# Layer 1's heads: the second map's scores half a step behind the first map's, with the first turns and the values between them

## The chip, the cores and the metric

The kernel runs on one core of one Trainium2 chip. A core has a matrix engine (PE, with its weight loads shown apart as PEld), a vector engine (DVE), a scalar engine (ACT), GpSimd (POOL) and SyncE (SP), which here only issues DMAs. Each engine works off its own list of instructions in order, and the engines wait for each other through semaphores. PE writes its results to eight banks of PSUM, from which DVE and ACT read. The metric is the device time of one execution in microseconds; lower is better.

## The reference

A backbone of two layers over 1024 latent tokens and 256 context tokens of width 1024. Layer 0 is a latent attention and isn't touched here. Layer 1 is a differential attention with 8 heads: each head has two attention maps over the 1280 keys, and one value of width 128.

```
def diff_mixer(h, h_c, rows, need_ctx, layer_idx, w_in, lam, g_sub):
    ...
    def combine(o1, o2, gate):
        o = o1 - lam_full.astype(o1.dtype) * o2
        o = rms_norm(o, g_sub) * (1.0 - lambda_init)
        return gated(o, gate)
    ...
    o1, o1_c = prefix_attention(q[:, :, :, 0:1], k[:, :, :, 0], v, ...)
    o2, o2_c = prefix_attention(q[:, :, :, 1:2], k[:, :, :, 1], v, ...)
```

Behind it come the output projection, a residual and a layer norm.

## The kernel before

Layer 1 runs head by head, and in a head by tiles of 128 query tokens: 8 steps of `step1` for each of the 8 heads. A step works on three tiles at once:

- **Scores** of the current tile (`scores1`, a generator with three parts). The first part computes the first map's scores and the scores of both maps against the context: on PE a bank for the context (four products 256 wide) and two banks of 512 keys (two products each, L1348 and L1349); on DVE the context's maxima (L1361), two maxima (L1365) and their combination (L1367); on ACT three exponentials (L1371) with their sums. The second part does the two 512-key banks of the second map and its three exponentials. The third part is DVE's alone: the sums (L1374), a reciprocal, a factor (L1376), and the **join** of both maps into one (L1377).
- **Turns** of the tile before (`turn1`, three calls): PE transposes the joined map, 4, 4 and 2 blocks of 128 (L1384), ACT rounds them to `ph` (L182) and DVE keeps the remainder as `pl` (L183).
- **Values** of the tile before that (`values1`): 30 products with `ph`, `pl` and the values on PE (L1392 to L1394), then `o` and its square sum on ACT (L1397, L1398), small work on POOL, and a DMA to `o_d`. Head 7 keeps its result in the chip.

Between these parts, `some(side, cost)` lets a generator with other work go on: for heads 0 to 6 the projections of the next head (k, q, then v, each product 256 or 512 wide, recorded at L186 to L188) with their weights (`wx`, `wy`), their rotation (`rsw`, `kr`, `rr`), rounding (`kH`, `kL`, `vh`, `vl`) and gates (`gg`); for head 7 the output projection of finished tiles. The cost counts streamed columns. `at` holds five costs: `SLOT1` is 2900 five times for heads 0 to 6, `SLOTO` is 0 and then 7000 four times for head 7. Head 7 has no side work in its first two steps.

PE's order is the order in which the code is written (a manual schedule for PE alone); the order on DVE, ACT, POOL and SP and the PSUM bank of each tile are chosen by a scheduler when the program is built. `HP` is 0. There are two buffers each of `ph`, `pl` and of the first map's `p0`, one of the second map's `p1`, four of `sm`.

Of the kernel before, what the change touches and what calls it, by code (L numbers as in the profile page):

```python
# [39 lines left out]
HP = 0  # L40
# [14 lines left out]
def hybrid_kernel(  # L55
# [33 lines left out]
    def bank(tag, dt=F32):  # L89
        return banks["pool"].tile([P, 512], dt, tag=tag, bufs=banks[tag], name=nm("ps_" + tag))  # L90
# [5 lines left out]
    def spool(name, **kw):  # L96
        return tc.tile_pool(name=name, bufs=1, reuse_waits="tile", **kw)
# [5 lines left out]
    def rot(pool_, shape, dt, tag, bufs=1, first=False):  # L103

        if not first and (id(pool_), tag) in pre:
            return pre.pop((id(pool_), tag))
        t = pool_.tile(shape, dt, tag=tag, bufs=bufs, name=nm(tag))
        if first:
            pre[id(pool_), tag] = t
        return t  # L110
# [48 lines left out]
    def rstd_of(dst, src, mul, n):  # L159
        pool.tensor_scalar(dst, src, mul, EPS, op0=ALU.mult, op1=ALU.add)  # L160
        pool.tensor_tensor(dst, dst, neghalf[:, :n], op=ALU.pow)
# [7 lines left out]
    hp = p0.enter_context(spool("p0"))  # L169
# [398 lines left out]
    def chain(*gs):  # L568
        for g in gs:
            yield from g  # L570

    def beside_gates():
        with spool("p0side") as sp_:
            for i, _ in enumerate(up_weights(sp_)):
                if i in (1, 3, 5, 7, 9, 13, 17):
                    yield
        with spool("p0side2") as sp_:
            t_ = lambda tag: sp_.tile([P, D], F32, tag=tag, bufs=3, name=nm(tag))
            yield
            yield  # L580
            yield from ada_dve(t_, ((1, 0), (1, 1), (0, 2)))
# [9 lines left out]
    with spool("p0g") as pg:  # L591
        side = beside_gates()
# [384 lines left out]
    def w1(tag):  # L977
        sh, d, b = TAG1[tag]
        return rot(place[tag], sh, d, tag, b)
# [250 lines left out]
    def weave(main, side, at):  # L1230

        for i, v in enumerate(main):
            if i in at:
                next(side, None)
            yield v
        yield from side
# [37 lines left out]
    def prod_q1(h, b, ps=None):  # L1274
        c0, n = CHUNKS[b]
        if ps is None:
            for ps in proj1(n, c0, slice(0, P)):
                yield 3 * n
        rr = w1("rr")
        c = slice(c0, c0 + n)  # L1280
        rope1(ps, n, cosB[:, c], sinB[:, c], rr)
        if b == 0:
            qt1[h] = [w1(f"Q1{m}") for m in range(2)], [w1(f"QS{m}") for m in range(2)]
        q1, qs = qt1[h]

        def fin():
            H, L = w1("kH")[:, :n], w1("kL")[:, :n]
            if b:
                split16(H, L, rr, es1[h])
            else:  # L1290
                act.activation(H, rr, AF.Copy, scale=es1[h])
                pool.tensor_scalar(rr, rr, es1[h], None, op0=ALU.mult)
                pool.tensor_tensor(L, rr, H, op=ALU.subtract)
            for m in range(2):
                r = slice(m * HD, m * HD + HD)
                dmv(qs[m][:HD, c], H[r, :])
                dmv(qs[m][HD:, c], H[r, :])
                dmv(q1[m][:HD, c], L[r, :])
                dmv(q1[m][HD:, c], L[r, :])

        later.append(fin)
        yield 0
# [85 lines left out]
    def values1(h, t, ph, pl, sm):  # L1388
        vh, vl = vt[h]
        ps = bank("b")[:, :P]  # L1390
        for kc in range(NT):
            pe.matmul(ps, ph[:, kc, :], vh[:, kc, :], start=kc == 0, stop=False)  # L1392
            pe.matmul(ps, ph[:, kc, :], vl[:, kc, :], start=False, stop=False)
            pe.matmul(ps, pl[:, kc, :], vh[:, kc, :], start=False, stop=kc == NT - 1)  # L1394
        o, o2, ss = w1("o1"), w1("o2"), w1("ss")
        pool.tensor_tensor(sm[:, 5:6], sm[:, 2:3], us1[h], op=ALU.mult)  # L1396
        act.activation(o, ps, AF.Copy, scale=sm[:, 5:6])  # L1397
        act.activation(o2, o, AF.Square, accum_out=ss[:, 0:1])  # L1398
        rstd_of(ss[:, 1:2], ss[:, 0:1], 1.0 / P, 1)
        if h == H1 - 1:  # L1400
            oo, g = og[t]
            c = slice(h * P, (h + 1) * P)
            dve.scalar_tensor_tensor(oo[:, c], o, ss[:, 1:2], g[:, c], op0=ALU.mult, op1=ALU.mult)
            return
        pool.tensor_scalar(o, o, ss[:, 1:2], None, op0=ALU.mult)
        sp.dma_start(o_d[1][t * P:(t + 1) * P, h * P:(h + 1) * P], o)
# [148 lines left out]
    def some(gen, cost):  # L1555

        credit[0] += cost
        while credit[0] > 0:
            v = next(gen, None)
            if v is None:  # L1560
                credit[0] = 0
                return
            credit[0] -= v

    with tc.manual_schedule(engines={ENG[c] for c in MAN1}):
        for _ in prod_q1(0, 0, made.pop("q")):
            pass
        later.pop()()
        for _ in chain(prod_k1(0, made), prod_q1(0, 1),
                       weave(prod_v1(0), prod_w(1, 0), WAT[1])):  # L1570
            while later:
                later.pop(0)()
        joined, turned = [], []

        def step1(cur, side, at):

            with tc.high_priority(HP):
                if cur:
                    S = scores1(*cur)
                    next(S)  # L1580
            some(side, at[0])
            with tc.high_priority(HP):
                if cur:
                    next(S)
                if turned:
                    values1(*turned.pop(0))
            some(side, at[1])
            pc = None
            if joined:
                c_, pc, sm = joined.pop(0)  # L1590
                ph, pl = w1("ph"), w1("pl")
                turned.append((*c_, ph, pl, sm))
            for (k0, n), v in zip(((0, 4), (4, 4), (8, 2)), at[2:]):
                if pc is not None:
                    with tc.high_priority(HP):
                        turn1(pc, ph, pl, k0, n)
                some(side, v)
            if cur:
                with tc.high_priority(HP):
                    joined.append((cur, *next(S)))  # L1600
            for _ in range(len(later)):
                later.pop(0)()

        def v_last(h):
            while later:
                later.pop(0)()
            out_early()
            yield from weave(prod_v1(h), chain(*[out_w1(k, lambda: w1("ws")) for k in range(NSP, NOW)],
                                               *[out_pre(k) for k in range(NOW, KT)]), range(1, 36, 2))

        g1 = gate_row1()
        part = lambda h: (v for _, v in zip(range(6 if h else 0), g1))
        early = lambda h: out_w1(h - 3, lambda: w1("ws")) if 3 <= h < 3 + NSP else iter(())
        for h in range(H1):
            last = h == H1 - 1
            if not last:
                G = chain(weave(weave(chain(prod_k1(h + 1), prod_q1(h + 1, 0), prod_q1(h + 1, 1)), part(h), (1, 6, 11, 16, 21, 26)),
                                prod_w(h + 1, 1), WAT[0]),
                          weave(weave(prod_v1(h + 1), early(h), (5, 15)), prod_w(h + 2, 0), WAT[1]) if h + 2 < H1 else v_last(h + 1))
            else:  # L1620
                while later:
                    later.pop(0)()
                out_open()
            for t in range(SEQ // P):
                if last:
                    if t >= 2:
                        out_load(t)
                    G = weave(out_tile1(t - 2), out_turns(t - 1), (9, 12)) if t >= 2 else iter(())
                    if t == 2:
                        G = chain(out_turns(0), G)  # L1630
                    credit[0] = 0
                step1((h, t), G, SLOT1 if not last else SLOTO)
                if last:
                    for _ in G:
                        pass
            for _ in G:
                pass
        for t in range(SEQ // P - 2, SEQ // P):
            G = weave(out_tile1(t), out_turns(t + 1), (9, 12))
            credit[0] = 0  # L1640
            step1(None, G, SLOTO)
            for _ in G:
                pass
# [74 lines left out]
```

## Time and profile before

| | us |
|---|---|
| three runs, median | 1769.6 |
| lowest and highest | 1768.27 and 1771.5 |
| the profiled execution's span, from its first to its last instruction | 1767.7 |
| its heads 0 to 6 of layer 1 | some 947 to 1600 |
| its head 7 and the end | some 1600 to 1767.7 |

The profile is of one execution. Its page gives the span and no other time of that execution; the median of the runs stands 1.9 us above the span. A row of a group gives the line, the engine, what is written and read, how many instructions there are, their busy time together, the mean in ns, and the engine's idle time ahead of them with what ended it. A row of a timeline gives the start, the duration, the engine and the line, and in square brackets an idle time ahead of it. Matmuls are pipelined: a 256-wide one is shown with 0.27 us, but the next starts 0.11 us later.

### The profile page before, as it was taken

What the parts mean: (1) busy time and instruction counts of PE and PEld (TensorE: products, weight loads), DVE (VectorE), ACT (ScalarE), POOL (GpSimd) and SP (SyncE); (2) the same over time, 40 slices, a digit from 0 to 9 for tenths busy, and PEclk for the clock granted to TensorE, in tenths of its full rate; (3) what the DMA queues carried; (4) which work ended last, traced back from release to release, by engine and by line L of the source; (5) the groups of instructions that cost most, each with busy time, mean ns of one, the idle gap of its engine ahead of it and who ended that gap; (6) DMA issues with size and microseconds to landing.
All of it is one profiled execution on the core that took longest, in us unless ns stands there. A gap on an engine that the chain in (4) does not pass through costs nothing. (4 is left out here: it accounts for less than half of the span.)

```text
span 1767.7 us, 36788 instructions
## 1 busy us (share of the span) xinstructions
PE 1660.4 (94%) x14564; PEld 1231.8 (70%) x14564; DVE 1224.6 (69%) x2037; ACT 1118.5 (63%) x2235; POOL 821.9 (46%) x740
## 2 busy tenths in 40 slices
PE   7999989999999998899999999999999999987998
PEld 6999956556666655577867676767676767666876
DVE  7658666565565666646856778787878787878664
ACT  3551177777777778845635676767676767758542
POOL 1432147667767776845552323241424233354454
PEclk9999999999999999999999999999999999999999
DMA  8258520110111122245522222231212222142331
GB/s 308 81 152 259 166 68 21 43 44 22 42 46 25 39 57 62 65 168 196 167 96 64 80 68 80 67 81 55 60 51 63 60 58 75 32 125 66 112 108 72
DMA packets 111225, 154.84 MB, mean 88 GB/s; under 512 B 13415, under 2 KB 84679, under 8 KB 111054
## 3 DMA queue, kind: packets, MB, share of 16 engines
q1 hardware_dynamic: 102654, 144.90, 27.3%
q10 hardware_dynamic: 8400, 7.61, 1.3%
q8 instruction: 114, 1.87, 0.4%
q14 instruction: 57, 0.47, 0.1%
HBM read 98.65 MB, written 27.07 MB: 71 GB/s over the span
## 5 line engine op out<-in xcount | busy, mean ns | idle before, releaser
L780 POOL TENSOR_TENSOR pl<-p,ph 128x1024 f16<-128x1024 f32 (+1 forms) x176 | 364.3, 2076 | 148.4 <-ACT ph L779 122.6
L1371 ACT ACTIVATE p<-ps_b,mx 128x512 f32<-128x512 f32 (+1 forms) x384 | 230.2, 617 | 58.9 <-DVE mx L1367 57.4
L778 ACT ACTIVATE p<-ps_a,esc 128x1024 f32<-128x1024 f32 (+1 forms) x176 | 189.0, 1074 | 94.8 <-PE ps_a L836 88.8
L760 DVE TENSOR_REDUCE mx<-ps_a 128x1 f32<-128x1024 f32 x128 | 155.3, 1222 | 129.9 <-PE ps_a L758 129.8
L779 ACT CAST ph<-p 128x1024 f16<-128x1024 f32 (+1 forms) x176 | 177.1, 1006 | 5.5
L1365 DVE TENSOR_REDUCE mx<-ps_b 128x1 f32<-128x512 f32 x256 | 164.9, 680 | 0.7 <-PE ps_b L1349 0.7
L849 PE MATMUL ps_d<-Vh,pl 128*128 128x65 f16 x1344 | 146.0, 194 | 4.4 <-POOL pl L780 4.4
L846 PE MATMUL ps_d<-Vh,ph 128*128 128x65 f16 x1344 | 148.2, 195 | 0.0
L848 PE MATMUL ps_d<-Vl,ph 128*128 128x64 f16 x1344 | 147.0, 193 | 0.0
L846 PEld LDWEIGHTS <-ph 128*128 128x128 f16 x1344 | 123.3, 97 | 18.1 <-issue 4.9
L848 PEld LDWEIGHTS <-ph 128*128 128x128 f16 x1344 | 124.0, 98 | 12.2 <-issue 0.3
L1348 PE MATMUL ps_b<-KS,QS 128*128 128x512 f16 (+1 forms) x384 | 126.5, 347 | 5.9 <-DVE pl L183 2.9
L1349 PE MATMUL ps_b<-KS,Q 128*128 128x512 f16 (+1 forms) x384 | 129.7, 347 | 0.0
L834 PE MATMUL ps_a<-qH,KH 100*128 100x512 f16 x320 | 121.9, 381 | 7.8 <-ACT p L778 3.5
L1396 POOL TENSOR_TENSOR sm<-sm,us 128x1 f32<-128x1 f32 x64 | 18.5, 289 | 234.3 <-DVE sm L1375 221.2
L849 PEld LDWEIGHTS <-pl 128*128 128x128 f16 x1344 | 123.2, 97 | 5.8 <-POOL pl L780 5.8
L1384 PE MATMUL ps_b<-idr,p 128*128 128x128 f32 x640 | 103.8, 278 | 24.2 <-ACT p L1371 6.2
L183 DVE SCALAR_TENSOR_TENSOR pl<-ps_b,lcf,ph 128x512 f16<-128x512 f32 (+1 forms) x192 | 116.9, 653 | 11.2 <-ACT ph L182 11.2
L182 ACT ACTIVATE ph<-ps_b,lcf 128x512 f16<-128x512 f32 (+1 forms) x192 | 115.2, 647 | 13.9 <-PE ps_b L1384 13.8
L835 PE MATMUL ps_a<-qH,KL 96*128 96x512 f16 x320 | 121.8, 381 | 0.0
L836 PE MATMUL ps_a<-qL,KH 96*128 96x512 f16 x320 | 121.2, 379 | 0.0
L1384 PEld LDWEIGHTS ps_b<-idr,p 128*128 128x128 f32 x640 | 78.2, 143 | 49.0 <-ACT p L1371 11.6
(438 smaller groups left out, 5290.7 us busy)
## 6 DMA issues: line engine op xcount, KB each, us to landing
ws<-in_dw SPq DMA_DIRECT2D x28, 512.0 KB, 3.9
adw<-in_ada_w SPq DMA_DIRECT2D x24, 512.0 KB, 4.6
adaw<-in_ada_w SPq DMA_DIRECT2D x16, 512.0 KB, 7.3
g<-sg_d SPq DMA_DIRECT2D x16, 512.0 KB, 8.5
sg_d<-gg ACTq DMA_DIRECT2D x40, 128.0 KB, 3.6
o_d<-op SPq DMA_DIRECT2D x7, 640.0 KB, 3.8
xt<-in_xT SPq DMA_DIRECT2D x16, 256.0 KB, 4.4
wgs<-in_w_in SPq DMA_DIRECT2D x32, 128.0 KB, 3.1
```

The source lines that it names most:

```text
L760: dve.tensor_reduce(mx[:, t, 0:1], ps, axis=AX.X, op=ALU.max)
L778: act.activation(p32[:, :n], st, AF.Exp, scale=esc0)
L779: act.copy(ph[:, :n], p32[:, :n])
L780: pool.tensor_tensor(pl[:, :n], p32[:, :n], ph[:, :n], op=ALU.subtract)
L846: pe.matmul(pv[:, t, :], ph[:, ts], Vh[:, k, h, :], start=(k == kcs[0] and t == 0), stop=False, skip_group_check=True)
L848: pe.matmul(pv[:, t, :V0], ph[:, ts], Vl[:, k, h, :], start=False, stop=False, skip_group_check=True)
L849: pe.matmul(pv[:, t, :], pl[:, ts], Vh[:, k, h, :], start=False, stop=(k == NT - 1), skip_group_check=True)
L1348: pe.matmul(out, qs[m][:, ts], ks[m][:, c0:c0 + n], start=True, stop=False)
L1349: pe.matmul(out, q1[m][:, ts], ks[m][:, c0:c0 + n], start=False, stop=True)
L1365: dve.tensor_reduce(mx[:, 2 + 2 * m + i:3 + 2 * m + i], b, axis=AX.X, op=ALU.max, negate=True)
L1371: act.activation(p[m][:, c0:c0 + n], b, AF.Exp, bias=nb, accum_out=sm[:, 2 + 3 * m + i:3 + 3 * m + i])
L1384: pe.transpose(st[:, j * P:(j + 1) * P], pc[:, (k0 + j) * P:(k0 + j + 1) * P], idn)
```

## The change

`step1` calls the same parts in another order. Before: scores of the first map, side work, scores of the second map, values, side work, then the three turns with side work behind each. Now: scores of the first map, side work, the first turn, side work, the values, scores of the second map, side work, then the second and the third turn with side work behind each. The join stays at the end.

```diff
-            with tc.high_priority(HP):
+            hp = lambda: tc.high_priority(HP)
+            pc = None
+            with hp():
                 if cur:
                     S = scores1(*cur)
                     next(S)
             some(side, at[0])
-            with tc.high_priority(HP):
-                if cur:
-                    next(S)
-                if turned:
-                    values1(*turned.pop(0))
-            some(side, at[1])
-            pc = None
             if joined:
                 c_, pc, sm = joined.pop(0)
                 ph, pl = w1("ph"), w1("pl")
+            old = turned.pop(0) if turned else None
+            if pc is not None:
                 turned.append((*c_, ph, pl, sm))
-            for (k0, n), v in zip(((0, 4), (4, 4), (8, 2)), at[2:]):
-                if pc is not None:
-                    with tc.high_priority(HP):
+            for i, (k0, n) in enumerate(((0, 4), (4, 4), (8, 2))):
+                if pc is not None and n:
+                    with hp():
                         turn1(pc, ph, pl, k0, n)
-                some(side, v)
+                some(side, at[1 + i])
+                if i == 0:
+                    with hp():
+                        if old:
+                            values1(*old)
+                        if cur:
+                            next(S)
+                    some(side, at[4])
             if cur:
-                with tc.high_priority(HP):
-                    joined.append((cur, *next(S)))
+                with hp():
+                    pc, sm = next(S)
+                    joined.append((cur, pc, sm))
```

How the rows move on three engines follows. In the names, `ps_b` is a PSUM bank, `QS`, `Q` and `KS` are the parts of queries and keys, `idr` is the identity of the transposes, and the numbers tell one tile from another.

First PE, in step 1 of head 0, behind the first slot of projections; `-` is before, `+` is now:

```order
 L188 MATMUL ps_b_12997<-h1H,wx_12835 128x512
-L1348 LDWEIGHTS QS_1871_12537
-L1348 MATMUL ps_b_13036<-KS_1879_12589,QS_1871_12537 128x512
-L1349 LDWEIGHTS Q_1869_12535
-L1349 MATMUL ps_b_13036<-KS_1879_12589,Q_1869_12535 128x512
-L1348 LDWEIGHTS QS_1871_12537
-L1348 MATMUL ps_b_13040<-KS_1879_12589,QS_1871_12537 128x512
-L1349 LDWEIGHTS Q_1869_12535
-L1349 MATMUL ps_b_13040<-KS_1879_12589,Q_1869_12535 128x512
+L1384 MATMUL ps_b_13038<-idr,p_1916_12929 128x128 x4
 L186 LDWEIGHTS wy_12885
```

The second map's scores leave this place, and the first turn of the joined map of step 0 (`p_1916`) takes it; from step 2 on the 30 products of the values go with the scores, behind the next slot.

Next DVE, around the start of head 4's scores. This is the order before, from the last tile of head 3 (`sm_16591`, joined into `p_2506`) to the first of head 4 (`mx_16753`):

```order
L1374 TENSOR_REDUCE sm_16591<-sm_16591 128x2
L1375 RECIPROCAL sm_16591<-sm_16591 128x2
L1376 SCALAR_TENSOR_TENSOR sm_16591<-sm_16591,nlam 128x1
L1377 SCALAR_TENSOR_TENSOR p_2506_16592<-p_2507_16593,sm_16591,p_2506_16592 128x1280
L183 SCALAR_TENSOR_TENSOR pl_16696<-ps_b_16697,lcf,ph_16695 128x512
L183 SCALAR_TENSOR_TENSOR pl_16696<-ps_b_16719,lcf,ph_16695 128x512
L183 SCALAR_TENSOR_TENSOR pl_16696<-ps_b_16732,lcf,ph_16695 128x256
L1361 TENSOR_REDUCE mx_16753<-ps_b_16757 128x2
L1365 TENSOR_REDUCE mx_16753<-ps_b_16763 128x1
L183 SCALAR_TENSOR_TENSOR vl_16054<-Vf_16052,kc_92,vh_16053 128x1280
```

And this is the order now at the same place:

```order
L183 SCALAR_TENSOR_TENSOR pl_16628<-ps_b_16719,lcf,ph_16627 128x512
L183 SCALAR_TENSOR_TENSOR pl_16628<-ps_b_16732,lcf,ph_16627 128x256
L1374 TENSOR_REDUCE sm_16591<-sm_16591 128x2
L1361 TENSOR_REDUCE mx_16753<-ps_b_16757 128x2
L1375 RECIPROCAL sm_16591<-sm_16591 128x2
L1365 TENSOR_REDUCE mx_16753<-ps_b_16763 128x1
L1376 SCALAR_TENSOR_TENSOR sm_16591<-sm_16591,nlam 128x1
L183 SCALAR_TENSOR_TENSOR vl_16054<-Vf_16052,kc_92,vh_16053 128x1280
L1377 SCALAR_TENSOR_TENSOR p_2506_16592<-p_2507_16593,sm_16591,p_2506_16592 128x1280
L1365 TENSOR_REDUCE mx_16753<-ps_b_16767 128x1
```

The join of head 3's last tile stood ahead of the next tile's maxima; now it stands behind the context's maximum, one more maximum and `vl`.

Last ACT, in step 6 of head 3. Before, the exponentials of both maps (`p_2484` the first, `p_2485` the second) stood together:

```order
L1371 ACTIVATE p_2484_16432,sm_16431<-ps_b_16440,mx_16430 128x512
L1371 ACTIVATE p_2484_16432,sm_16431<-ps_b_16444,mx_16430 128x512
L1371 ACTIVATE p_2484_16432,sm_16431<-ps_b_16434,mx_16430 128x256
L1371 ACTIVATE p_2485_16433,sm_16431<-ps_b_16467,mx_16430 128x512
L1371 ACTIVATE p_2485_16433,sm_16431<-ps_b_16471,mx_16430 128x512
L1371 ACTIVATE p_2485_16433,sm_16431<-ps_b_16434,mx_16430 128x256
L182 ACTIVATE ph_16526<-ps_b_16528,lcf 128x512
```

Now the second map's stand behind the values' work, with other instructions among them:

```order
L1326 COPY Vf_16052<-ps_b_16454 128x128
L1328 COPY gg_16051<-ps_b_16454 128x128
L1326 COPY Vf_16052<-ps_b_16543 128x128
L994 ACTIVATE wsq_17002,sq_16870<-ws_16873 128x1024
L182 ACTIVATE ph_16467<-ps_b_16556,lcf 128x512
L1371 ACTIVATE p_2485_16433,sm_16431<-ps_b_16523,mx_16430 128x512
L182 ACTIVATE ph_16467<-ps_b_16575,lcf 128x256
L1371 ACTIVATE p_2485_16433,sm_16431<-ps_b_16527,mx_16430 128x512
L1326 COPY Vf_16052<-ps_b_16549 128x128
L1328 COPY gg_16051<-ps_b_16549 128x128
L1371 ACTIVATE p_2485_16433,sm_16431<-ps_b_16434,mx_16430 128x256
```

Two roundings of turned blocks, four copies of the value projection and a square sum have come ahead of the last exponential of the second map or between them.

## The prediction

> **What bounds the kernel now.** I read the page first, then the busy time by stretches, the waits of PE, and a timeline of single instructions, since the change touches only the heads of layer 1.
>
> ```profile
> span 1767.7 us, 36788 instructions
> PE 1660.4 (94%) x14564; PEld 1231.8 (70%) x14564; DVE 1224.6 (69%) x2037; ACT 1118.5 (63%) x2235; POOL 821.9 (46%) x740
> ```
>
> The changed code runs from 947 us to the end. These are busy times in that stretch; the columns are PE, PEld, DVE, ACT, POOL, then the granted clock.
>
> ```profile
> 947.00:1600.00 653.00, 617.40 (x5177) 447.88 (x5176) 517.21 (x1006) 455.08 (x1246) 219.48 (x325) 0.99 0.23 66
> 1600.00:1625.00 25.00, 18.14 (x166) 13.56 (x163) 20.97 (x34) 23.50 (x55) 12.78 (x10) 0.86 0.33 109
> 1625.00:1650.00 25.00, 22.73 (x160) 17.73 (x161) 18.57 (x36) 12.30 (x35) 9.24 (x13) 1.00 0.21 62
> ```
>
> In heads 0 to 6 PE is idle for 653.0 - 617.4 = **35.6 us**, or 5.1 us a head; that is the most the change can win there. DVE is busy 79% and ACT 70% of the stretch. PE waits for many small things, hardly for the join (L1377):
>
> ```profile
> PE ps_b L1384 <- ACT p L1371: 6.2, 13, 1.5
> PE ps_b L186 <- DVE pl L183: 6.2, 5, 1.3
> PE ps_b L1384 <- ACT rr L1314: 5.9, 3, 2.3
> PE ps_b L186 <- ACT p L1371: 4.3, 11, 0.8
> PE ps_b L1384 <- DVE p L1377: 2.6, 3, 2.0
> ```
>
> So PE is the bound, and what feeds the first turn has slack. The question is how much slack the new order leaves.
>
> **The change, part by part.** No instruction is added or removed. Call S1 the first map's scores (with the context's), S2 the second map's, T1 to T3 the turns, V the values, all on PE, whose order is the program's. Durations, from the rows below: S1 lasts 1.30 us (1311.89 to 1313.19), a projection slot of twelve 256-wide products 1.31 (1313.19 to 1314.50), S2 0.86 (1314.50 to 1315.36).
>
> ```profile
> 1311.89 0.27 PE L1348 MATMUL ps_b<-KS,QS 128*128 128x256 f16 x1
> 1313.19 0.27 PE L186 MATMUL ps_b<-wx,h1H 128*128 128x256 f16 x1
> 1314.50 0.38 PE L1348 MATMUL ps_b<-KS,QS 128*128 128x512 f16 x1
> 1315.36 0.22 PE L1392 MATMUL ps_b<-vh,ph 128*128 128x128 f16 x1
> ```
>
> Before, T1 turned the joined map of the preceding step only after that step's V and four slots, and then S1, a slot, S2, V and another slot: some 14 us after the S2 that feeds it (S2, V, five to six slots, the turns and both scores of the next step). Now V and S2 stand behind T1. From S2 to T1 there remain S2, three slots, T2, T3 (0.65 together), S1 and one slot. **T1 now stands 2.60 us behind the start of S1**, and S1 4.1 to 5.4 us behind the preceding S2, since some slots are half as long: 6.7 to 8.0 us from S2 to T1. V and T2, T3 gain or keep their distance.
>
> How long does the path from S2 to T1 take? A lightly loaded step shows its links:
>
> ```profile
> 1316.25 1.28 DVE L1365 TENSOR_REDUCE mx<-ps_b 128x1 f32<-128x512 f32 x2
> 1317.56 0.27 DVE L1367 TENSOR_SCALAR mx<-mx 128x1 f32<-128x1 f32 x1
> 1318.15 0.69 ACT L1371 ACTIVATE p<-ps_b,mx 128x512 f32<-128x512 f32 x1
> 1319.83 0.23 ACT L1371 ACTIVATION_READ_ACCUMULATOR p<-ps_b,mx 128x1 f32 x1
> 1320.09 0.16 DVE L1374 TENSOR_REDUCE sm<-sm 128x2 f32<-128x6 f32 x1 [2.26 <-ACT p L1371]
> 1320.74 1.55 DVE L1377 SCALAR_TENSOR_TENSOR p<-p,sm,p 128x1280 f32<-128x1280 f32 x1
> 1321.02 1.64 ACT L182 ACTIVATE ph<-ps_b,lcf 128x512 f16<-128x512 f32 x3
> ...
> 956.67 0.27 PE L1349 MATMUL ps_b<-KS,Q 128*128 128x256 f16 x1
> 956.98 0.69 DVE L1361 TENSOR_REDUCE mx<-ps_b 128x2 f32<-128x512 f32 x1 [0.43 <-PE ps_b L1349]
> 1053.36 1.54 DVE L1377 SCALAR_TENSOR_TENSOR p<-p,sm,p 128x1280 f32<-128x1280 f32 x1
> 1055.05 0.63 PE L1384 MATMUL ps_b<-idr,p 128*128 128x128 f32 x4 [0.29 <-DVE p L1377]
> ```
>
> From the start of S2: its second chunk ends at 1.03, two maxima and L1367 end at 2.3, the exponentials start at 2.4. The three of them take 1.91 (1318.15 to 1320.06), and the new order on ACT puts two ph of the turns between them, some 1.0 (1.64 is three): done at 5.35. Sum, reciprocal and factor take 0.65 (1320.09 to 1320.74), the join 1.55, join to turn 0.15 (1054.90 to 1055.05): **7.7 us with nothing else in the queues**, as much as the new distance.
>
> But there is more in the queues. In the new DVE order the context's maximum of the next step (L1361) stands ahead of the join in nearly every step, and it can't begin before S1 is 0.64 old (four products to 0.60, then 0.04 as at 956.94 to 956.98). So by the DVE rows alone T1 starts at 0.64 + 0.61 + what stands between + 1.55 + 0.15 behind S1. What stands between differs by the step; the long ones have these rows:
>
> ```profile
> L183 DVE SCALAR_TENSOR_TENSOR vl<-Vf,kc,vh 128x1280 f16<-128x1280 f32 x7 | 10.8, 1543 | 1.0 <-ACT vh L182 1.0
> L183 DVE SCALAR_TENSOR_TENSOR kL<-rr,es,kH 128x512 f16<-128x512 f32 x7 | 6.6, 940 | 4.2 <-ACT kH L182 3.6 <-DMA Q<-kL 0.6
> L994 ACT ACTIVATE wsq<-ws 128x1024 f32<-128x1024 f32 x23 | 25.2, 1095 | 10.4 <-DMA ws<-in_dw 10.4
> L182 ACT ACTIVATE vh<-Vf,kc 128x1280 f16<-128x1280 f32 x7 | 9.8, 1402 | 0.0
> L1326 ACT COPY Vf<-ps_b 128x128 f32<-128x128 f32 x65 | 19.7, 303 | 6.3 <-PE ps_b L188 6.3
> ```
>
> The eight steps of a head, worked by these durations (a maximum 0.60, a small operation 0.15 to 0.25 apart): what stands between L1361 and the join; T1 behind S1 by that list alone; the exponentials' end behind S1 (5.35, plus what else ACT's order has among them, less the distance S2 to S1); T1 by both.
>
> | step | between | by DVE's list | exponentials end | T1 by both |
> |---|---|---|---|---|
> | 0 | reciprocal, maximum, factor, vl (waits for ACT's vh) | 5.45 | 1.2, vh at 3.3 | 6.4 |
> | 1 | factor, maximum | 3.8 | 0 | 3.8 |
> | 2 | two small ones | 3.2 | 0.5 | 4.0 |
> | 3 | reciprocal, two maxima, factor | 4.6 | 1.8 (wy, kH, wsq ahead) | 5.9 |
> | 4 | kL, factor, maximum | 4.65 | 0.7 | 5.0 |
> | 5 | nothing | 2.95 | 1.2 (Vf, gg) | 4.2 |
> | 6 | nothing | 2.95 | 0.4 | 3.4 |
> | 7 | sum, two maxima, the rest | 5.0 | 2.1 (Vf, gg twice, wsq) | 5.8 |
> | sum | | 32.6 | | 38.5 |
>
> PE reaches T1 at 8 x 2.60 = 20.8 in a head. It waits 32.6 - 20.8 = 11.8 us a head by DVE's list alone, 38.5 - 20.8 = **17.7 us** with ACT. S2 stands behind T1, so that a late T1 makes the next S2 late too: the wait comes back in every step and isn't made up. I take 17.7, nearest to the timeline's links; 11.8 is the lower end. For the upper end I take the longest path that the trace shows, below in the rivals.
>
> The sum: 7 x 17.7, less 3.8 for the first step, which has no turn, is 120. The waits of today go, as PE then comes late to everything else: -35.6. The last head's first steps have no projections as cover: between S2 and T1 lie T2, T3 and S1 (2.8 us where 7.7 or more are needed) at steps 1 and 2, and out_open's work stands ahead of the first join; I reckon 19 us where PE is idle 6.9 + 2.3 = 9.1 now, **+10**. From step 2 on 7000 units stand in each slot, longer than the path: nothing. The values come later, but only the last head reads what L1406 writes, and L1396 to L1405 are small on a POOL that is busy 219 of 653 us: nothing. Two buffers of ph and pl suffice for the new order, since V of the older tile was over a step before.
>
> **The clock.** A wait also has a price behind it:
>
> ```profile
> 1187.81 0.66 PE L1384 MATMUL ps_b<-idr,p 128*128 128x128 f32 x4 [2.10 <-ACT rr L1314]
> 1187.00:1192.00 5.00, 4.19 (x23) 3.44 (x24) 1.11 (x4) 4.97 (x19) 1.37 (x3) 0.66 0.23 58
> 1580.00:1585.00 5.00, 4.20 (x24) 3.00 (x23) 2.20 (x4) 4.56 (x16) 3.80 (x3) 0.66 0.00 0
> ```
>
> A wait of 2.10 us cost 5 x (1 - 0.66) = 1.7 us of clock. Steps 0, 3 and 7 wait over 3 us, 20 times in all; two of three, 14, at 1.7, less three of that kind today, give **+19**; none and all 20 are the ends, -5 and +29. The Trainium skill, TensorE: Matmul & The Clock Gate, Part 1, halves the clock after an idle window of about 3.4 us; by that only step 0 would pay, 7 x 1.7 - 5 = +7 in the place of +19. The row with 2.10 us speaks against so long a window.
>
> Total: 120 - 35.6 + 10 + 19 = +113. The profiled span becomes 1767.7 + 113 = 1881; the median shown stands 1.9 above the span, so **1883 us**.
>
> **Rivals.**
> 1. DVE's list alone binds and ACT is always in time: 7 x 11.8 - 3 - 35.6 = +44, and with half of the other terms some 1770 + 44 + 15 = 1829. For it: the fastest paths. Chance 0.17.
> 2. The path is as long as where DVE and ACT are laden now. Quickest and slowest:
>
> ```profile
> 1267.23 0.38 PE L1348 MATMUL ps_b<-KS,QS 128*128 128x512 f16 x1
> 1282.31 1.54 DVE L1377 SCALAR_TENSOR_TENSOR p<-p,sm,p 128x1280 f32<-128x1280 f32 x1
> ```
>
> From S2 to the join's end 16.6 us here, 7.8 at 1314.50 to 1322.29; the middle, 12.2, over an allowed 7.4 gives 4.8 x 55 = 264 - 36 = +228, 1998 us. Against it: of these 16.6 us much is the first map's exponentials, which stand between S2 and the second map's now and no longer then. Between this and the forecast lies 1930 to 2000. Chance 0.13.
> 3. Faster: S2 half a step later asks for its two banks when the first map's are free, so PE's waits for ACT's p go, and the join is done in time. Won at most 35.6: 1734 us. It decides if the join ends before S1 + 2.45, that is if nothing but L1361 stands ahead of it and ACT is done by S1; only steps 6 and 5 come near. Chance 0.07.
> 4. The waits only move from the banks to the turns, some 5 us a head either way: 1770 us. Chance 0.03.
>
> **How the numbers follow.** The forecast, 1840 to 1930 us, has 0.60, with 1883 as its centre. The range is **1808 to 1945**: it takes in rival 1, whose term is +44 with nothing else, and the start of rival 2, and leaves out rivals 3 and 4 and most of 2, some 2 in 10. About 0.2% is what a measurement of this kernel can tell from no change. Slower 0.90, same 0.03, faster 0.07.
>
> **What would show it.** Right: PE waits at L1384 for DVE p L1377 by 80 to 130 us in heads 0 to 6; the step grows from 653 / 56 = 11.7 to some 13.3 us; the longest waits at steps 0, 3 and 7; more stretches of half clock. Wrong: PE's idle time in the heads stays under 45 us, or the waits end on another line (ph, a bank, a projection's weight); then the list was right but the path shorter, or the banks were the bound.

## The result, and the profile after

The changed kernel takes **1933.0 us** (median of 4 runs, 1926.9 to 1937.1), the kernel before 1769.1 beside it: ratio 1.0924, 95% interval 1.0899 to 1.095. It is slower by 9%, inside the range, 50 us above the forecast.

The page of the changed kernel, its span and its engines:

```profile
span 1928.9 us, 36789 instructions
PE 1700.1 (88%) x14564; PEld 1255.3 (65%) x14564; DVE 1244.5 (65%) x2037; ACT 1135.5 (59%) x2235; POOL 816.2 (42%) x740
```

The span grew by 161.2 us with the same number of matmuls. To see where, here is the busy time by stretches, cut at the first scores of head 0 and of head 7. Before the change head 7 starts at 1606.31 us, not at 1600. The columns are the length, then PE, PEld, DVE, ACT, POOL, then the granted clock, the DMA engines' share and their GB/s. Before:

```profile
947.70:1606.31 658.61, 623.01 (x5240) 453.16 (x5238) 521.04 (x1013) 460.95 (x1265) 221.44 (x328) 0.99 0.23 65
1606.31:1767.70 161.39, 143.73 (x936) 113.06 (x933) 104.00 (x197) 79.95 (x195) 78.38 (x79) 0.96 0.29 98
```

After:

```profile
950.23:1736.93 786.70, 651.80 (x5241) 471.01 (x5238) 535.71 (x1010) 476.78 (x1262) 213.18 (x328) 0.95 0.20 54
1736.93:1928.90 191.97, 150.90 (x936) 116.42 (x933) 107.88 (x200) 80.44 (x199) 79.74 (x78) 0.92 0.25 82
```

Heads 0 to 6 take 128.1 us more: PE's idle time goes from 658.61 - 623.01 = 35.6 to 134.9 us (+99.3), and the same products take 28.8 us longer at the lower clock. Head 7 and the end take 30.6 more. The other 2.5 us lie ahead of the heads.

PE's waits in heads 0 to 6 (us in total, times, longest), to be read against the list of small waits before:

```profile
PE ps_b L1384 <- DVE p L1377: 100.4, 43, 5.6
PE ps_b L1384 <- ACT p L1371: 15.4, 4, 4.9
PE ps_b L1384 <- DVE uw L1006: 9.0, 5, 1.8
PE ps_b L1348 <- ACT p L1371: 8.1, 4, 3.4
```

125 of 135 us are the first turn's own. The rows with p L1371 and uw L1006 are the same wait under the names of other operations that end near the join: in 52 of the 53 waits the first turn starts 0.06 to 0.15 us behind the join's end, whatever the row names. The bank waits of before are gone but for some 2 us, as the prediction had it, and one of another kind came (L1348 on p, 8.1): S1's bank is still read by exponentials that ran late.

Two steps of the changed kernel show how the turn is held up, in the timelines of DVE and PE at a step 5 and a step 0; in brackets stands the idle time ahead and what ended it:

```profile
1256.61 0.16 DVE L1374 TENSOR_REDUCE sm<-sm 128x2 f32<-128x6 f32 x1
1257.14 0.68 DVE L1361 TENSOR_REDUCE mx<-ps_b 128x2 f32<-128x512 f32 x1
1257.74 1.54 DVE L1377 SCALAR_TENSOR_TENSOR p<-p,sm,p 128x1280 f32<-128x1280 f32 x1
1259.42 0.63 PE L1384 MATMUL ps_b<-idr,p 128*128 128x128 f32 x4 [0.74 <-DVE p L1377]
...
1295.92 0.68 DVE L1361 TENSOR_REDUCE mx<-ps_b 128x2 f32<-128x512 f32 x1
1297.43 1.55 DVE L183 SCALAR_TENSOR_TENSOR vl<-Vf,kc,vh 128x1280 f16<-128x1280 f32 x1
1298.90 1.55 DVE L1377 SCALAR_TENSOR_TENSOR p<-p,sm,p 128x1280 f32<-128x1280 f32 x1
1300.59 1.09 PE L1384 MATMUL ps_b<-idr,p 128*128 128x128 f32 x4 [2.99 <-DVE p L1377]
```

DVE is never idle between L1361 and the join; the next step's maximum, at step 0 also vl, stands ahead of it. The turn of step 0 runs 1.09 us, the one of step 5 0.63: behind the 2.99 us wait the clock is down (0.73 of full speed granted from 1298 to 1303 us).

The same by step, in us: T1's wait, forecast (the prediction's table less 2.60) and measured, mean over heads 0 to 6 of the profiled execution (step 0: heads 1 to 6).

| step | 0 | 1 | 2 | 3 | 4 | 5 | 6 | 7 | sum |
|---|---|---|---|---|---|---|---|---|---|
| forecast | 3.8 | 1.2 | 1.4 | 3.3 | 2.4 | 1.6 | 0.8 | 3.2 | 17.7 |
| measured | 3.0 | 1.9 | 1.4 | 3.7 | 3.6 | 0.9 | 0.8 | 3.1 | 18.3 |

Head 7's new waits: the first from the timelines of PE and DVE, the other two from the list of waits from 1790 us on.

```profile
1747.55 3.60 DVE L1377 SCALAR_TENSOR_TENSOR p<-p,sm,p 128x1280 f32<-128x1280 f32 x1
1751.29 1.09 PE L1384 MATMUL ps_b<-idr,p 128*128 128x128 f32 x4 [12.90 <-DVE p L1377]
...
PE ps_b L188 <- DVE wy L178: 8.0, 5, 1.7
PE ps_b L1497 <- DVE ws L1403: 2.7, 2, 1.7
```

The first join waits behind out_open's work, as forecast. The other two were not. What makes the one at L188 shows in DVE's timeline at step 4 of head 7, whose scores start at 1663.54 us before and at 1811.96 now. Before:

```profile
1674.65 0.35 DVE L1403 SCALAR_TENSOR_TENSOR ws<-o,ss,g 128x128 f32<-128x128 f32 x1 [5.49 <-POOL ss L161]
1675.56 1.55 DVE L1377 SCALAR_TENSOR_TENSOR p<-p,sm,p 128x1280 f32<-128x1280 f32 x1
1678.35 1.34 DVE L178 TENSOR_TENSOR wy<-ps_b,wx 128x512 fp32r<-128x512 f32 x3
```

After, with PE's row last:

```profile
1823.25 0.35 DVE L1403 SCALAR_TENSOR_TENSOR ws<-o,ss,g 128x128 f32<-128x128 f32 x1 [3.08 <-POOL ss L161]
1823.52 0.68 DVE L1365 TENSOR_REDUCE mx<-ps_b 128x1 f32<-128x512 f32 x1
1827.13 1.55 DVE L1377 SCALAR_TENSOR_TENSOR p<-p,sm,p 128x1280 f32<-128x1280 f32 x1
1829.27 1.34 DVE L178 TENSOR_TENSOR wy<-ps_b,wx 128x512 fp32r<-128x512 f32 x3
1830.20 0.50 PE L188 MATMUL ps_b<-o,wy 128*128 128x512 f32 x1 [1.74 <-DVE wy L178]
```

The last column of the tile (L1403) comes at the same place as before, 11.1 and 11.3 us behind the scores. But a maximum of the second map's late scores now stands behind it, the join comes 3.1 us later, and the split (L178) that the step's last products need stands behind the join.

### The profile page after: what moved, and what is told of

Same layout as the page of the kernel before. It is cut to its first block, busy times and chain, and to the rows that moved or that the text cites. A ratio compares the mean times of both kernels' runs of the same rounds, so it can differ in the third digit from the quotient of the medians.

```text
span 1928.9 us, 36789 instructions
## 1 busy us (share of the span) xinstructions
PE 1700.1 (88%) x14564; PEld 1255.3 (65%) x14564; DVE 1244.5 (65%) x2037; ACT 1135.5 (59%) x2235; POOL 816.2 (42%) x740
## 4 chain that ended last, share of the span: by engine, by line
PE 43%; DVE 26%; ACT 13%; DMA 6%; POOL 6%; issue 5%; SPq 1%; POOLq 0%; ACTq 0%; DVEq 0%
DVE mx L1365 4%; DVE p L1377 4%; DMA ws<-in_dw 4%; ACT p L1371 3%; PE ps_a L834 3%; PE ps_a L835 3%; PE ps_a L836 3%; PE ps_b L188 3%; PE ps_b L186 3%; PE ps_a L186 3%; PE ps_b L187 3%; PE ps_a L188 3%; PE ps_a L187 3%; PE ps_a L758 2%; DVE pl L183 2%
## 5 line engine op out<-in xcount | busy, mean ns | idle before, releaser
L1371 ACT ACTIVATE p<-ps_b,mx 128x512 f32<-128x512 f32 (+1 forms) x384 | 234.2, 617 | 85.1 <-DVE mx L1367 84.9
L1384 PE MATMUL ps_b<-idr,p 128*128 128x128 f32 x640 | 109.6, 289 | 147.1 <-DVE p L1377 122.1
L183 DVE SCALAR_TENSOR_TENSOR pl<-ps_b,lcf,ph 128x512 f16<-128x512 f32 (+1 forms) x192 | 125.9, 657 | 121.2 <-ACT ph L182 121.2
L160 POOL TENSOR_SCALAR ss<-ss 128x1 f32<-128x1 f32 x64 | 13.1, 205 | 398.4 <-ACT o L1398 397.6
L1348 PE MATMUL ps_b<-KS,QS 128*128 128x512 f16 (+1 forms) x384 | 127.6, 349 | 9.6 <-ACT p L1371 8.1
```

Source lines behind the costliest of these rows:

```text
L1371: act.activation(p[m][:, c0:c0 + n], b, AF.Exp, bias=nb, accum_out=sm[:, 2 + 3 * m + i:3 + 3 * m + i])
L1384: pe.transpose(st[:, j * P:(j + 1) * P], pc[:, (k0 + j) * P:(k0 + j + 1) * P], idn)
```

## The experiments

The theory: what costs is the distance in PE's order from the second map's scores (S2) to the first turn (T1) that they feed, against a path through exponentials, sums and join that runs on two in-order lists. Rivals: the new places cost by themselves; the banks; the clock alone.

**e1: S2 back, T1 early.** One of the two moves undone.

```diff
-            for i, (k0, n) in enumerate(...):
-                ...
+            if cur: next(S)                # S2
+            if pc is not None: turn1(pc, ph, pl, 0, 4)
+            some(side, at[1])
+            if old: values1(*old)
+            some(side, at[4])
+            ... turn1(4, 4), slot, turn1(8, 2), slot
```

> The second map's scores go back to their place of before (first map, slot, second map); the first turns stay where the change has them, ahead of the values. So one of the change's two moves is kept (turns early), the other undone. From the second map's scores to the first turn that they feed lie then about 12.3 us of PE's own order instead of the changed kernel's 6.7 to 8.0. Theory (the distance on PE from the second map's scores to the next first turn is shorter than the path exponentials, sums, join): the waits of L1384 for DVE p L1377 fall from 122 us to under 15, time 1765 to 1795 us. Rival 'early turns': that the first turns stand ahead of the values is what costs: at least half of the loss stays, over 1850 us. Rival 'clock alone': the same as the theory here.

1806.9 us, ratio 1.020 (1.0178 to 1.0222). **e2: the complement.** S2 half a step late, T1 behind it.

```diff
+            if old: values1(*old)
+            some(side, at[1])
+            if cur: next(S)                # S2
+            if pc is not None: turn1(pc, ph, pl, 0, 4)
+            some(side, at[4])
+            ... turn1(4, 4), slot, turn1(8, 2), slot
```

> The complement: the second map's scores stay half a step behind the first map's, behind the values, and the first turns stand behind them (first map, slot, values, slot, second map, first turns, slot, other turns). From the second map's scores to the first turn that they feed lie about 12.3 us again. Theory: waits of L1384 for DVE p L1377 under 15 us, time 1755 to 1795 us. Rival 'half-step-late scores' (exponentials and join of the second map, pushed among ph, pl and the turns' work on ACT and DVE, cost by themselves, wherever the turns stand): at least half of the loss stays, over 1850 us.

1816.8 us, ratio 1.0264 (1.0245 to 1.0282). T1's waits for the join, e1's row first, then e2's:

```profile
PE ps_b L1384 <- DVE p L1377: 22.0, 14, 3.4
```

```profile
PE ps_b L1384 <- DVE p L1377: 21.9, 8, 4.2
```

Each undoes 71 to 77% of the loss, so neither move alone makes it; only together do they bring T1 near S2. Both missed the upper end of their expectation (1795 us): the waits for the join stay over 15 us, in e1 the turns also wait 24.9 us for pl, and e2's head 7 still takes 190 us, where e1's takes 169. In the first three steps of head 7 it takes both moves: 40.3 us before, 43.8 in e1, 44.1 in e2, 55.8 in the changed kernel. From step 3 on the loss follows S2 and not the values. In e1 the values stand later than in the changed kernel (6.1 us behind the scores at step 4, there 5.2), the join at 10.3, and L188 waits for no wy; steps 3 to 6 take 17.2 us each (17.0 before). In e2 the values stand early (1.3 us), S2 late, the join at 17.6, and these steps take 19.8 to 22.5 us (19.2 to 19.8 in the changed kernel). Late values cost at the very end: e1 keeps 2.6 us of waits for L1403 there.

**e3: the join in two pieces.**

```diff
-        dve.scalar_tensor_tensor(p[0], p[1], sm[:, 4:5], p[0], ...)
+        for c in (slice(0, 512), slice(512, NTOK)):
+            dve.scalar_tensor_tensor(p[0][:, c], p[1][:, c], sm[:, 4:5], p[0][:, c], ...)
```

> The changed kernel with its join (L1377) written in two pieces, columns 0 to 512 and 512 to 1280. T1 turns only the first 512, so it can start about 0.9 us (1280 less 512 columns of 1.55 us) earlier in each of the 55 steps in which it waits; nothing else moves. Theory: the waits of L1384 for the join fall by 0.6 to 0.9 us a step, 33 to 50 us, and the clock gives 5 to 25 us back with them: 1860 to 1895 us. Rival 'not the join's end but the exponentials or ACT end the wait': no change, 1920 to 1945 us. The same if the release is kept by whole tiles and T1 waits for both pieces.

1916.9 us, ratio 1.0828: 16 us faster, less than expected. By step, T1's wait falls by the same 0.80 us wherever DVE's list is the whole story: 2.99 to 2.19 at step 0 (four heads of six), 1.81 to 1.01 at step 1, 1.80 to 1.00 at step 2, 0.88 to 0.08 at step 6, 0.73 to nothing at step 5. So the join's end does release T1. But the edit also moves the lists that the scheduler builds: in heads 1 and 2 ACT now has the second map's last exponential behind vh, the gates (L1333) and the next map's exponentials, and step 0 waits 6.77. Steps 3, 4 and 7 together fall only from 73 to 66 us; there DVE and ACT also wait for loads (in head 2 ACT 6.57 us for L994's weights at step 4, DVE 2.71 for the gate row's at step 7), and e10 takes up one of these. The clock gave nothing back: half clock takes 92.2 us of heads 0 to 6, 81.9 in the changed kernel.

**e4: the slot between T1 and V moved ahead of T1.**

```diff
-SLOT1 = 2900, 2900, 2900, 2900, 2900
+SLOT1 = 5800, 0, 2900, 2900, 2900
```

> The changed kernel with the projection slot that stands between T1 and V moved ahead of T1 (the slots' sizes are 5800, 0, 2900, 2900, 2900 instead of five of 2900); the work is the same. T1 stands then about 1.3 us (a full slot; 0.65 a half one) later behind the first map's scores. Theory: T1's waits shrink by 0.7 to 1.3 us a step, 40 to 70 us, and the clock gives 10 to 30 us back: 1835 to 1885 us. Rival 'the waits only move' (the slot's own products wait for something that the turns waited for, or the wait stands at the next line): no more than 20 us faster, over 1910 us.

1899.0 us, ratio 1.0727, between theory and rival: T1's waits fall by 25 us in place of 40 to 70. As in e3, ACT's list moves and two heads wait long at step 0 (7.4 and 6.7 us), and half clock stays at 81.9 us.

**e6: the order of before in head 7 only.**

```diff
+        def step_old(cur, side, at):
+            ...
-                step1((h, t), G, SLOT1 if not last else SLOTO)
+                (step_old if last else step1)((h, t), G, SLOT1 if not last else SLOTO)
```

> The changed order in heads 0 to 6, the order of before in head 7 and in the drain after it. Heads 0 to 6 should stay as in the changed kernel (about 787 us from the first scores to head 7's). Theory (head 7's 30.6 us come from its own order: first turns with 2.8 us of cover at its first steps, and values that run some 3.5 us later behind a 7000 slot, so that the last column's turn ends the step): head 7 to the end goes back from 192 to 161 to 172 us, time 1902 to 1914 us. Rival 'it is the late join that heads 0 to 6 leave behind, or out_open's work': head 7 stays over 182 us, time over 1922 us.

1907.3 us, as expected in the time. This edit moves S2, T1 and V back together, so it doesn't tell them apart; by e1 and e2 the values' part of the expectation's reason doesn't hold. In its stretches the heads stay, and head 7 comes back by 26.8 of the 30.6 us:

```profile
953.06:1740.62 787.56, 652.99 (x5240) 472.04 (x5238) 536.30 (x1010) 476.30 (x1262) 212.66 (x328) 0.95 0.20 54
1740.62:1905.80 165.18, 142.54 (x936) 113.33 (x933) 106.20 (x200) 80.83 (x199) 75.45 (x78) 0.95 0.30 95
```

**e7: products that feed nothing inside the waits.** They add work that the reference doesn't have.

```diff
         st = bank("b")
+        if fill:
+            for _ in range(8):
+                pe.matmul(st, qt1[fill - 1][1][0][:, :P], kt1[fill - 1][0][:, :512], start=True, stop=True)
```

> The changed kernel with eight products of 128x512 (some 1.8 us of PE, of scores' operands, into the bank that the first turns overwrite) ahead of the first turns at steps 0, 3, 4 and 7 of heads 0 to 6, where PE waits 2.8 us or longer anyway; they add work and feed nothing. Theory (the clock is halved by these waits, and costs about half of 82 us in heads 0 to 6): the filler lies inside the waits and shortens them to 1 to 3 us, half clock falls from about 82 us to 20 to 50, time 1900 to 1922 us although PE does 27 x 1.8 = 49 us more. Rival 'the clock has nothing to do with these waits, or costs nothing since the waits take up what it loses': 1930 to 1950 us. Should the waits be bound by PE's own pace and not by the join: up to 1933 + 49 = 1982 us.

1919.0 us, ratio 1.0824 (1.0797 to 1.085): 14 us faster with 216 more products. Its heads:

```profile
950.50:1722.80 772.30, 678.66 (x5456) 478.99 (x5455) 537.84 (x1010) 475.13 (x1262) 212.78 (x328) 0.98 0.20 56
```

The clock's records show 30.7 us of half clock in these heads, 81.9 in the changed kernel. PE's idle time falls by 41 us, the filler takes some 47 (216 x 0.216), and the products of the kernel run 20 us faster. The waits bring the low clock, and it is a cost of its own.

**e9: S2 still half a step late, T1 a full slot behind it.** Head 7 as before.

```diff
-SLOT1 = 2900, 2900, 2900, 2900, 2900
+SLOT1 = 2900, 1450, 2900, 2900, 1450, 2900
+            if old: values1(*old)
+            some(side, at[1])
+            if cur: next(S)                # S2
+            some(side, at[2])
+            ... turn1(0, 4), slot, turn1(4, 4), slot, turn1(8, 2), slot
```

> The second map's scores half a step behind the first map's, behind the values, as in the changed kernel, but the first turns a full slot behind the second map's scores (first map, slot, values, half slot, second map, slot, first turns, slot, second turns, half slot, third turns, slot) in heads 0 to 6; head 7 as before. From the second map's scores to the first turn that they feed lie about 13.8 us. Theory (only the distance counts; half-step-late scores cost nothing by themselves): waits of L1384 for DVE p L1377 in heads 0 to 6 under 10 us, heads 0 to 6 in 640 to 670 us (658.6 before), time 1750 to 1785 us. Rival 'half-step-late scores cost by themselves': heads 0 to 6 over 675 us, time over 1790 us.

1775.4 us, ratio 1.0026 (1.0015 to 1.0037); the heads take 663.0 us (658.6 before). The waits for the join are 12.5 us, a little over the 10 that were expected. With all that moves in this order, the net cost is 4.4 us.

**e10: no gate row.** The gate row's eight loads and multiply-adds (L1420) are left out.

```diff
-        for k in range(KT):
+        for k in range(0):
             w = w1("ws")
             sp.dma_start(w, ada_w[1, k * P:(k + 1) * P, 2 * D:3 * D])
```

> The changed kernel without the gate row's eight weight loads and their eight multiply-adds on DVE (L1420) in heads 0 to 3: this part of the computation is left out. Theory of a second chain (these loads share the three ws buffers with the projection's weights; the multiply-adds stand behind the late join on DVE, so the weights are loaded late, ACT's L994 waits for them 5 to 7 us in heads 0 to 3, and the exponentials queued behind it come late): heads 0 to 3 fall from 460.6 us towards the 434 us that four heads like 4 to 6 take, time 1900 to 1915 us. Rival 'the load is late for another reason, or ACT's stall is hidden': heads 0 to 3 lose under 12 us (the multiply-adds alone are 8 x 1.53), time over 1920 us.

1902.0 us in one run: heads 0 to 3 fall from 461.4 to 430.6 us, 19 us more than the multiply-adds' own 12. What they do shows in the changed kernel's head 2, step 3 to 4, in the timelines of DVE, SP, ACT and PE:

```profile
1226.82 1.52 DVE L1420 SCALAR_TENSOR_TENSOR gate<-ws,sc,gate 128x1024 f32<-128x1024 f32 x1
1232.54 0.53 SPq L990 DMA_DIRECT2D ws<-in_dw  x1
1236.63 1.06 ACT L994 ACTIVATE wsq<-ws 128x1024 f32<-128x1024 f32 x1 [5.34 <-DMA ws<-in_dw]
1239.08 0.59 PE L1348 MATMUL ps_b<-KS,QS 128*128 128x512 f16 x1 [3.41 <-ACT p L1371]
1246.37 1.09 PE L1384 MATMUL ps_b<-idr,p 128*128 128x128 f32 x4 [3.42 <-DVE p L1377]
```

The multiply-add stands right behind the late join (1225.18 to 1226.72) and holds one of the three ws buffers until 1228.3; SP issues the next weights' load at 1232.54, behind the gate's load and eight stores of q. ACT reaches L994 and stands still for 5.34 us, and the second map's exponentials are queued behind it. In e10 the same load goes out right behind the same store of o, 5.7 us after the load before it and not 17.6:

```profile
1205.54 0.45 SPq L990 DMA_DIRECT2D ws<-in_dw  x1
```

ACT's wait for it over heads 0 to 3, in the changed kernel and then in e10:

```profile
ACT wsq L994 <- DMA ws<-in_dw: 33.8, 12, 7.2
```

```profile
ACT wsq L994 <- DMA ws<-in_dw: 9.9, 9, 2.2
```

T1 behind S1 at step 4 of heads 0 to 3 goes from 9.0, 11.3, 11.3 and 8.2 us to 6.1, 6.1, 6.1 and 5.8: a second chain, through SP and a DMA. Over heads 0 to 6, T1's waits fall by 7.7 us, S1's by some 6, and the rest of the 27.6 us is the clock (half clock 51.2 us in place of 81.9). Whether the buffer or the place in SP's queue makes the load late wasn't tried apart.

**e11: T1 between the maps, but one step later.** Head 7 as before.

```diff
-            if joined:
+            if len(joined) > two[0]:       # 1 in heads 0 to 6, then 0
-        p = [w1("p0"), w1("p1")]
+        p = [w1("p0c" if (8 * h + t) % 3 == 2 and h < H1 - 1 else "p0"), w1("p1")]
```

> The changed kernel's order of PE in heads 0 to 6, the first turns still between the two maps' scores, but they turn the map joined two steps before instead of one (a third p0 buffer; the values follow a step later, one step without scores drains it ahead of head 7, which has the order of before). From the second map's scores to the first turn that they feed lie about 18.4 us of PE's order instead of 7.5. To make room, L994 writes its squares 16 bits wide and the heads' small output tiles have one buffer less. Theory (nothing but the distance costs): waits of L1384 for DVE p L1377 in heads 0 to 6 under 5 us instead of 100, heads 0 to 6 in 640 to 672 us, time 1750 to 1785 us; under 1765 it would beat the kernel before, if the banks' waits of today go with it. Rival 'the places themselves cost' (second scores half a step late, turns between): heads 0 to 6 over 690 us, time over 1800 us.

1802.0 us, ratio 1.0208 (1.0179 to 1.0237): a miss in time, though the heads lie in the range (671.2 us). T1 waits for no join there; the longest waits of PE are these:

```profile
PE ps_b L1348 <- DVE pl L183: 11.4, 9, 2.3
PE ps_b L1348 <- ACT rr L1314: 9.6, 5, 3.3
PE ps_b L1348 <- ACT p L1371: 8.2, 10, 1.0
```

So with distance enough the new places, and the buffers that had to change, cost 12.6 us net of the 128, in waits for banks. The heads start 9.6 us later than before and the end takes 6.9 more; which of the added buffers does that wasn't tried.

**e12: T1 behind V, directly ahead of S2.** Head 7 as before.

```diff
+            if old: values1(*old)
+            some(side, at[1])
+            if pc is not None: turn1(pc, ph, pl, 0, 4)
+            if cur: next(S)                # S2
+            some(side, at[2])
+            ... turn1(4, 4), slot, turn1(8, 2), slot
```

> A dose between: in heads 0 to 6 the first turns stand behind the values and directly ahead of the second map's scores (first map, slot, values, slot, first turns, second map, slot, second turns, slot, third turns, slot), head 7 as before. From the second map's scores to the first turn that they feed lie 10.4 us, between the changed kernel's 7.5 (heads 0 to 6: 787 us), 8.75 (756) and 11.7 (675 and 687). Theory (the loss falls with the distance): PE reaches T1 5.6 us behind the first map's scores, so only steps 3, 4 and 7 still wait, some 28 us, and with clock and banks heads 0 to 6 take 685 to 720 us, time 1797 to 1833 us. Rival 'the turn's place ahead of the second scores is what costs, since a late turn makes the next scores late': over 740 us in the heads, over 1850 us.

1801.5 us, ratio 1.0192 (1.0167 to 1.0217); heads 686.3 us, waits for the join 21.2: as expected in size, and the rival falls. They stand mostly at steps 0 and 7 though (8.3 and 5.9 us at T1), not at 3, 4 and 7. The orders side by side, in us (the distance from PE's order by the prediction's durations, mean of heads 1 to 6; it is 0.6 to 0.8 less than the expectations of e1, e2 and e9 say):

| kernel | S2 to T1 | T1 for the join, heads 0 to 6 | heads 0 to 6 |
|---|---|---|---|
| after | 7.5 | 100.4 | 786.7 |
| e4 | 8.75 | 87.8 | 755.8 |
| e12 | 10.4 | 21.2 | 686.3 |
| e1 | 11.7 | 22.0 | 687.0 |
| e2 | 11.7 | 21.9 | 674.8 |
| e9 | 13.0 | 12.5 | 663.0 |
| before | 14.6 | 5.2 | 658.6 |
| e11 | 18.4 | 0 | 671.2 |

The loss falls with the distance by and large, not in every row: e1 and e2 differ by 12 us at the same 11.7, and e11 stands above the kernel before. Places, banks and DVE's and ACT's lists are worth that much.

**e13 and e14: a dose of work ahead of the join**, in the changed kernel and in the one before.

```diff
+        dve.tensor_scalar(p[1][:, 0:768], p[1][:, 0:768], 1.0, None, op0=ALU.mult)
         dve.scalar_tensor_tensor(p[0], p[1], sm[:, 4:5], p[0], ...)
```

> The changed kernel with one more instruction on DVE between the second map's exponentials and the join: the first 768 columns of p1 times 1.0, some 0.45 to 0.9 us. Theory (no slack between the join and the first turns): the waits grow by the instruction's length in nearly every step of heads 0 to 6, 48 x 0.45 to 0.9 = 22 to 43 us, and the clock takes up to 15 us more: 1950 to 1990 us. Rival 'the join isn't what the turns wait for, PE or ACT sets the pace': under 1943 us.

> The kernel before with the same instruction in the same place. Theory (14.6 us from the second scores to the turns against a path of 7 to 16, 11.9 in the mean, so that only step 4 has no slack): 7 x 0.45 to 0.9 = 3 to 6 us at most and little else, 1767 to 1779 us. Rival 'DVE's load itself is the bound': as much as in the changed kernel, over 1790 us.

e13 takes 1967.7 us, +34.6, as expected; e14 takes 1798.3, +30.2 and not under 10: the theory's total missed there. By step it is plain why. Without step 4, e14's other seven steps sum to 565.6 us over the heads, 569.7 before: they have slack, the dose (0.71 us each) is free. In the changed kernel steps 0, 1, 2, 5 and 6 go from 447.5 to 470.3, +22.8 for 34 x 0.71 = 24. T1's waits make 16.0 of this, the clock the rest, and only steps 0 and 6 (+0.73 and +0.85 a wait) take the whole dose; step 2 takes none. By its total e14 lands where the rival had it (over 1790 us); the steps speak against the rival, since e14's step 4 alone goes from 88.9 to 120.2. Its rows, a wait of V and DVE's timeline in head 4:

```profile
PE ps_b L1393 <- DVE pl L183: 25.8, 5, 5.8
```

```profile
1394.14 1.29 DVE L1434 SCALAR_TENSOR_TENSOR ws<-ws,gsub,gate 128x1024 f32<-128x1024 f32 x1 [7.24 <-DMA ws<-in_out_w]
1395.41 1.14 DVE L183 SCALAR_TENSOR_TENSOR pl<-ps_b,lcf,ph 128x512 f16<-128x512 f32 x2
```

DVE reaches an instruction whose load hasn't landed, and two pl that V needs stand behind it. In heads 0 to 2 the load is the gate row's (4.8 to 6.9 us), in heads 4 and 5 the one shown. The dose moved DVE's list, and the list met a DMA: another cost than the one meant, but again an in-order engine before a late load.

## Why the prediction was right, and where it was not

- **The cause: right.** S2 and T1 came too near for the path between them. e1, e2, e9, e11 and e12 show it for heads 0 to 6: the loss falls with the distance, whichever move makes it, to within some 13 us.
- **The table of steps: right** in its sum (17.7 a head forecast, 18.3 measured), partly by luck: steps 0 and 5 were 0.8 and 0.7 too long, steps 1 and 4 0.7 and 1.2 too short. The longest are 3, 4 and 7, with 0 next. DVE's list with L1361 ahead of the join is confirmed where nothing else acts: e3 takes 0.80 us a step off there, and e13 puts 16.0 us of waits on over those steps.
- **T1's waits: 120 forecast, 125 measured.** Not in the sum were 9.5 us at the next S1, whose bank the late exponentials still read.
- **Step 4 was mis-sized** (2.4 against 3.6 us, and 3.4 more at S1 in heads 1 and 2). The table counted L994 on ACT as its own 1.1 us. Behind a late join the weights come late, and ACT stands before L994 for up to 7.2 us. Without that, in e10, step 4 still waits 3.1 us; what makes this remainder wasn't traced.
- **The clock: +19 forecast, +28.8 measured** in PE's busy time. There were 17 waits over 3 us, where 20 were forecast, but 29 over 2 us, and the shorter ones pay too (last section). The rule of the Trainium skill (TensorE: Matmul & The Clock Gate, Part 1), by which the prediction let only step 0 pay, gave +7 (+5 with the six heads whose step 0 has a turn); the trace has 81.9 us of half clock in heads 0 to 6 against 10.2, so the step that used the rows was nearer. e7 shows that it is worth removing.
- **Head 7's first steps: +10 forecast, +15.5 measured** (steps 0 to 2 go from 40.3 to 55.8 us). T1 waits 21.7 us there, where 19 were reckoned; the lower clock, 0.79 in the mean, wasn't counted.
- **"From step 2 on nothing": wrong.** Steps 3 to 6 cost 9.7 us and step 7 with the end 5.4. The argument asked whether a slot covers S2's path to the next turn. It does, but other work stands behind that path on DVE's list: the join comes late, and the split (L178) behind it holds up the step's last products. "The values come later: nothing" was right for steps 3 to 6, as e1 shows, and wrong at the end, where waits of 2.7 us for L1403 stand.
- **Rivals.** The result lies between DVE's list alone (1829) and the full laden path (1998). Faster and unchanged are out.

The forecast was low by 161 - 113 = 48 us: head 7 20.6, S1's waits 9.5, the clock 9.8, T1 5.3, the start 2.5.

No version here beats the kernel before; the nearest, e9, is 0.26% slower.

## What to carry to other kernels

In a software pipeline on in-order engines, measure a move by the distance in work between producer and consumer, and compare it with the path as it is queued, not as it runs alone: here the path from the second scores to the join's end took 7.1 to 16.6 us in the kernel before, and a distance of 13.0 us cost 4 us, 10.4 cost 28, 8.75 cost 97 and 7.5 cost 128. Look then for instructions on the feeding engines that wait for a load which is itself issued late; they turn a small delay into a large one. Follow also what stands behind the moved work on the other engines' lists: in head 7 PE had cover enough for the join, but not for the small split queued behind it.

## What the runs showed of the hardware that was not expected

**The granted clock.** It falls in pieces: in the changed kernel's records the low stretches last 3.41 us or a multiple (the last one, cut off by the end, aside). Over the 14 profiled executions, in heads 0 to 6, half clock came with 7 of 149 waits of 1.2 to 2.0 us, 15 of 38 of 2.0 to 2.5, 46 of 79 of 2.5 to 3.3, and 76 of 90 of longer ones. This looks like chance, but the same traces show a rule. In each execution all edges of the low stretches but that last one lie on one grid of 3.413 us, to 3 ns. Heads 0 to 6 cut along the grid give 2773 pieces at full clock. Of the 2634 in which PE stood idle for under 2.0 us, 6 were followed by half clock, and these 6 had over 1.8; of the 139 with 2.0 us or more, 138 were. So what counts is not a wait's length but how much idle time falls into one piece of the grid: a wait of 2.5 us that lies across an edge can be free. The Trainium skill, TensorE: Matmul & The Clock Gate, Part 1, says that the window is 3413 ns long and runs freely. The traces agree in both; here a window didn't have to be idle all through, 2.0 of its 3.41 us were enough.

**DVE behind POOL.** The join, 1.53 to 1.55 us everywhere else in the changed kernel, took 3.60 us once at head 7's start (the row above), while POOL ran a 128x1024 operation beside it. In the 13 traces in which the join is one instruction, 44 joins began while POOL was inside a tensor_tensor 512 or more wide, and all 44 ended 1.34 to 1.35 us behind that operation's end. The 8 that began inside a POOL tensor_scalar 512 wide took their 1.55 us. So the join seems to stand until such a POOL operation is over; no run was made to test this by itself.
